# An eight-phase trunk on one core: the order of the program from another timing model

## The chip, the cores and the metric

The kernel runs on one core of a Trainium2 chip. The metric is the device time of one execution in microseconds (us). TensorE (PE) multiplies matrices, VectorE (DVE) and ScalarE (ACT) do elementwise work and reductions, GpSimd (POOL) makes masks, and SyncE (SP) issues the DMAs. Each engine takes its instructions strictly in the order of the program for that engine and waits by semaphores for the others.

## The reference

512 tokens of width 1024 pass through eight sublayers. Each is `x + post_gain * rms_norm(f(rms_norm(x)))`, with these `f` in order: FFN, gated DeltaNet, cross-attention to 256 memory tokens, FFN, FFN, SSD (Mamba-2), cross-attention, FFN. The FFN is a SwiGLU of inner width 2816. The two recurrences, cut to what matters:

```python
# gated DeltaNet, per head and chunk
sol = triangular_solve(eye + a_mat, rhs, lower=True, unit_diagonal=True)
u, wk = sol[..., :dv], sol[..., dv:]
v_new = u - wk @ state
o = (qc * exp(G)) @ state + qk @ v_new
state = state * exp(G_end) + k_end.T @ v_new
...
o = rms_norm(o, norm_g) * silu(z);  return o @ w_out

# SSD, per group and chunk
y = (cb * seg) @ xc + (cc @ state) * exp(acum)
state = state * exp(acum_end) + (bc * to_end).T @ xc
...
yz = rms_norm((y + xs * d_skip) * silu(z), per group);  return yz @ w_out
```

All of it is float32.

## The kernel before

`trunk` makes a list of eight phases and `run` walks through it. The hidden state lies in SBUF with tokens on partitions; in front of each phase `features` (L244 to L250) or the FFN's `enter` (L373 to L382) normalises, transposes on PE and splits the result in two float32r parts, `xh` and `xl`. Every weight block of 128 x 1024 is loaded by one DMA of 512 KB into `raw` (three buffers), cast on ACT to `whi` (L129) and subtracted on DVE to `wlo` (L130; five buffers of each). A projection is then three float32r matmuls for each of eight blocks of the contraction (`mm3`, lines L143, L144, L145), into a PSUM bank. There are eight banks: three of tag `a`, two of `s`, two of `c`, one of `f`.

DeltaNet handles its 16 heads in eight pairs. For pair `p`, `front` (L659 to L716) makes masks and decays, `blocks` (L728 to L735) inverts 16 x 16 diagonal blocks on DVE, between two trips through DRAM, and `solve` (L748 to L795) puts the inverse together with small matmuls (L751, L760, L766, L771, L781, L788, L794). `scan` (L813 to L867) then runs four chunks of 128 tokens in sequence: L820 applies the state `S`, L826 the inverse `U`, L835 and L837 make the output, L845 the new state. At its end stand the sum of squares (L858), a reciprocal root of eleven small DVE steps (`rsqrt`, L307 to L312), the scaling (L867), and in `gate` four transposes for each head (L889), the product with `z` (L890) and the split into `oghi` and `oglo` (L893), which are the operands of the out projection. Between `solve(p)` and `scan(p)` the program writes the four projections of pair `p + 1`, eight blocks of three matmuls each, and the projections for `z` behind.

SSD has eight groups with the same frame: the scan's matmuls are L1068, L1071 and L1082, and its gate multiplies by `z` (L1108), squares (L1112), takes a root, scales (L1116) and transposes (L1120) into `sohi` and `solo`.

The order of the instructions is not the order in which they are written. The framework collects all instructions and schedules them: among those that are ready in its own model of time it takes the one with the lowest priority number, which counts up through the program. The kernel shifts these numbers for whole functions: the table `LATER` gives an offset for each name, and the decorator `prio` applies it while the function is written. What is ready when follows from a timing model of the engines. On each engine the program then holds that order, and waits, buffers and semaphores are set by it.

## Time and profile before

| what | value |
|---|---|
| median of 3 runs | 2835.14 us (2828.82 to 2835.72) |
| profiled execution | 2833.57 us |
| its span | 2831.8 us |
| mean granted clock of PE | 0.993 |
| PE busy | 2785.9 us, 98% |
| DVE, ACT, POOL busy | 2071.3, 1512.9, 124.5 us |
| HBM traffic | 112 GB/s over the span |

A row of the timeline gives the start in us, the duration in us, the engine, the line, the operation, `out<-in`, the form and, with `x2`, how many alike follow each other; in brackets stands the idle time ahead of it and what ended it. Matmuls are pipelined: their durations overlap, and the distance between two starts is what one costs. A row of a view of waits gives the waiting line, the one it waited for, and then the sum in us, the number of times and the longest. A row of the view by stretches gives the stretch and its length, then the busy time and count of PE, PE's weight loads, DVE, ACT and POOL, then PE's granted clock, the DMA share and GB/s.

### The profile page before, as it was taken

What the parts mean: (1) busy time and instruction counts of PE and PEld (TensorE: products, weight loads), DVE (VectorE), ACT (ScalarE), POOL (GpSimd) and SP (SyncE); (2) the same over time, 40 slices, a digit from 0 to 9 for tenths busy, and PEclk for the clock granted to TensorE, in tenths of its full rate; (3) what the DMA queues carried; (4) which work ended last, traced back from release to release, by engine and by line L of the source; (5) the groups of instructions that cost most, each with busy time, mean ns of one, the idle gap of its engine ahead of it and who ended that gap; (6) DMA issues with size and microseconds to landing.
All of it is one profiled execution on the core that took longest, in us unless ns stands there. A gap on an engine that the chain in (4) does not pass through costs nothing.

```text
span 2831.8 us, 45624 instructions
## 1 busy us (share of the span) xinstructions
PE 2785.9 (98%) x17648; PEld 2453.5 (87%) x17648; DVE 2071.3 (73%) x4057; ACT 1512.9 (53%) x2814; POOL 124.5 (4%) x141
## 2 busy tenths in 40 slices
PE   8999999999999999999999999999999999999998
PEld 7999987788888887999988999888888888799997
DVE  8887777767666564887778887777667766588776
ACT  5444477666575574544445444576554656454433
POOL 0000001000000000000000000003212200000000
PEclk9999999999999999999999999999999999999999
DMA  6333433232323432433343332433233363233233
GB/s 215 106 105 105 160 111 103 62 100 81 94 71 121 168 116 73 143 100 102 97 156 127 98 112 90 152 121 108 85 104 106 103 217 112 75 113 112 93 109 105
DMA packets 125913, 320.71 MB, mean 113 GB/s; under 512 B 27472, under 2 KB 46672, under 8 KB 125184
## 3 DMA queue, kind: packets, MB, share of 16 engines
q1 hardware_dynamic: 125696, 317.80, 34.6%
q8 instruction: 139, 2.28, 0.3%
q14 instruction: 78, 0.64, 0.1%
HBM read 293.01 MB, written 24.74 MB: 112 GB/s over the span
## 4 chain that ended last, share of the span: by engine, by line
PE 86%; DVE 7%; ACT 3%; DMA 2%; issue 1%; SPq 0%; DVEq 0%; POOL 0%; ACTq 0%; POOLq 0%
PE ps_a L143 16%; PE ps_a L144 16%; PE ps_a L145 16%; PE ps_s L144 4%; PE ps_s L145 4%; PE ps_s L143 4%; PE ps_c L143 2%; PE ps_c L145 2%; PE ps_c L144 2%; PE ps_f L145 2%; PE ps_f L144 2%; PE ps_f L143 2%; DVE wlo L130 1%; PE ps_c L1068 1%; PE ps_s L1237 1%
## 5 line engine op out<-in xcount | busy, mean ns | idle before, releaser
L143 PE MATMUL ps_a<-xh,whi 128*128 128x256 f32 (+1 forms) x2368 | 754.8, 321 | 2.0 <-ACT xh L381 1.7
L144 PE MATMUL ps_a<-xl,whi 128*128 128x256 f32 (+1 forms) x2368 | 755.4, 320 | 0.1
L145 PE MATMUL ps_a<-xh,wlo 128*128 128x256 f32 (+1 forms) x2368 | 752.3, 319 | 0.0
L143 PEld LDWEIGHTS ps_a<-xh,whi 128*128 128x128 f32 x2368 | 453.5, 192 | 30.3 <-ACT xh L381 2.6
L144 PEld LDWEIGHTS ps_a<-xl,whi 128*128 128x128 f32 x2368 | 455.0, 192 | 26.4 <-DVE xl L382 0.5
L145 PEld LDWEIGHTS ps_a<-xh,wlo 128*128 128x128 f32 x2368 | 454.4, 192 | 23.9
L130 DVE TENSOR_TENSOR wlo<-raw,whi 128x1024 fp32r<-128x1024 f32 x278 | 339.8, 1224 | 159.2 <-ACT whi L129 157.2
L129 ACT CAST whi<-raw 128x1024 fp32r<-128x1024 f32 x278 | 289.1, 1043 | 224.5 <-PE ps_a L144 139.1
L137 ACT CAST whi<-h 128x1024 fp32r<-128x1024 f32 x168 | 175.6, 1048 | 204.3 <-PE ps_a L144 150.3
L138 DVE TENSOR_TENSOR wlo<-h,whi 128x1024 fp32r<-128x1024 f32 x168 | 205.3, 1224 | 88.7 <-ACT whi L137 87.7
L492 ACT CAST bh<-raw 128x512 fp32r<-128x512 f32 x80 | 49.7, 621 | 169.0 <-DMA raw<-ffn_in 140.5
L144 PE MATMUL ps_s<-wlo,hhi 128*128 128x512 f32 x352 | 138.0, 392 | 0.0
L143 PE MATMUL ps_s<-whi,hhi 128*128 128x512 f32 x352 | 137.8, 392 | 0.0
L145 PE MATMUL ps_s<-whi,hlo 128*128 128x512 f32 x352 | 137.2, 390 | 0.0
L143 PE MATMUL ps_c<-whi,hhi 128*128 128x512 f32 x288 | 112.0, 389 | 0.0
L144 PE MATMUL ps_c<-wlo,hhi 128*128 128x512 f32 x288 | 112.0, 389 | 0.0
L145 PE MATMUL ps_c<-whi,hlo 128*128 128x512 f32 x288 | 112.0, 389 | 0.0
L137 ACT CAST whi<-raw 128x1024 fp32r<-128x1024 f32 x80 | 84.0, 1051 | 50.3 <-PE ps_c L145 39.0
L485 DVE TENSOR_TENSOR h<-raw 128x512 f32<-128x512 f32 x80 | 55.1, 689 | 72.1 <-DMA raw<-ffn_in 69.4
L138 DVE TENSOR_TENSOR wlo<-raw,whi 128x1024 fp32r<-128x1024 f32 x80 | 97.4, 1218 | 8.7 <-ACT whi L137 8.7
L512 ACT ACTIVATE h<-h 128x512 f32<-128x512 f32 x80 | 50.6, 633 | 84.3 <-DVE h L509 84.1
L468 ACT CAST hhi<-h 128x512 fp32r<-128x512 f32 x88 | 54.8, 622 | 71.7 <-DVE h L513 43.6
(423 smaller groups left out, 6635.4 us busy)
## 6 DMA issues: line engine op xcount, KB each, us to landing
raw<-ffn_in SPq DMA_DIRECT2D x192, 512.0 KB, 4.2
raw<-ffn_out SPq DMA_DIRECT2D x88, 512.0 KB, 3.5
raw<-dn_in SPq DMA_DIRECT2D x48, 512.0 KB, 3.5
raw<-ssd_in SPq DMA_DIRECT2D x32, 512.0 KB, 3.5
hd<-h SPq DMA_DIRECT2D x24, 512.0 KB, 3.1
h<-hd SPq DMA_DIRECT2D x24, 512.0 KB, 4.2
raw<-dn_out SPq DMA_DIRECT2D x16, 512.0 KB, 3.6
raw<-xa_k SPq DMA_DIRECT2D x16, 512.0 KB, 3.9
```

The lines of the kernel that those rows point to most:

```text
L129: nc.scalar.copy(hi[:, :n], raw[:, :n])
L130: nc.vector.tensor_sub(lo[:, :n], raw[:, :n], hi[:, :n])
L137: nc.scalar.copy(hi, raw)
L138: nc.vector.tensor_sub(lo, raw, hi)
L143: mm(ps, lhs[0], rhs[0], start=first, stop=False)
L144: mm(ps, lhs[0], rhs[1], start=False, stop=False)
L145: mm(ps, lhs[1], rhs[0], start=False, stop=last)
L468: self.t.nc.scalar.copy(hi, x)
L485: sub(T1, u[:, a], g[:, a])
L492: nc.scalar.copy(b22[0], u[:, b])
L512: nc.scalar.activation(gt, gt, AF.Silu)
L1068: nc.tensor.matmul(py[:, e * 64:e * 64 + 64], st["gp"][e][:, c, :], st["xt"][:, c, e * 64:e * 64 + 64], start=True, stop=True)
```

## The change

One argument of the tile context changes. The timing model that the scheduler consults while it orders the program is now the framework's timeline simulation of the engines, and no longer its default model.

```diff
--- before.py
+++ after.py
@@ -1425,7 +1425,7 @@
     nc = _bacc.Bacc("TRN2", target_bir_lowering=False, num_devices=1)
     ap = {n: nc.dram_tensor(n, list(x.shape), F32, kind="ExternalInput").ap() for n, x in arrays.items()}
     ap["out"] = nc.dram_tensor("out", [T, D], F32, kind="ExternalOutput").ap()
-    with tile.TileContext(nc) as tc:
+    with tile.TileContext(nc, schedule_with_timeline_sim=True) as tc:
         trunk(tc, nc, ap)
     res = run_bass_kernel_spmd(nc, [arrays], core_ids=[0])
     return np.asarray(res.results[0]["out"]).reshape(1, T, D)
```

The instructions are the same by name and number: 16552 matmuls, 4054 on DVE, 2392 on ACT, 136 on POOL and 677 DMAs. Only ACT's loads of function tables, which are put in once the order stands, go from 96 to 75. On PE 54% of the matmuls keep their place, the others move by 20 places in the mean and by some 300 at most; on DVE 21%, on ACT 25%, on SP 59% keep theirs. A small matmul is followed by a projection's matmul 524 times in the order before and 261 times now.

PE, the scan of DeltaNet's pair 1, before (names are `out<-weights and data`; `w`, `we`, `o`, `S` belong to the scan, `xh`, `xl`, `whi`, `wlo` to projections):

```order
L837 MATMUL ps_c<-w,gp 128x128 x2
L845 MATMUL ps_c<-we,ktok 128x256
L143 MATMUL ps_a<-xh,whi 128x512
L145 MATMUL ps_a<-xh,wlo 128x512
L144 MATMUL ps_a<-xl,whi 128x512
L143 MATMUL ps_a<-xh,whi 128x512
L145 MATMUL ps_a<-xh,wlo 128x512
L820 MATMUL ps_c<-S,u 128x256
```

The same scan now:

```order
L837 MATMUL ps_c<-w,gp 128x128 x2
L845 MATMUL ps_c<-we,ktok 128x256
L820 MATMUL ps_c<-S,u 128x256
L826 MATMUL ps_c<-o,U 128x128 x2
L835 MATMUL ps_c<-S,u 128x256
L837 MATMUL ps_c<-w,gp 128x128 x2
L845 MATMUL ps_c<-we,ktok 128x256
```

The projections that stood between the steps have moved ahead of the scan. At the end of pair 0's scan, just ahead of this, L889 now follows the last L837 with nothing between, as in the next place.

PE, the end of pair 7's scan, the last of DeltaNet, before (62 projection matmuls, most of them on the memory tokens of the following phase, stand between L837 and the first L889; here are the first of them):

```order
L835 MATMUL ps_c<-S,h 128x256
L145 MATMUL ps_a<-xh,wlo 128x256
L143 MATMUL ps_a<-xh,whi 128x256
L144 MATMUL ps_a<-xl,whi 128x256
L145 MATMUL ps_a<-xh,wlo 128x256
L143 MATMUL ps_a<-xh,whi 128x256
L144 MATMUL ps_a<-xl,whi 128x256
L145 MATMUL ps_a<-xh,wlo 128x256
L837 MATMUL ps_c<-w,gp 128x128 x2
L143 MATMUL ps_a<-xh,whi 128x256
```

And now (`oghi` is the output of the gate, so the last row is the out projection):

```order
L845 MATMUL ps_c<-we,ktok 128x256
L820 MATMUL ps_c<-S,h 128x256
L826 MATMUL ps_c<-o,U 128x128 x2
L835 MATMUL ps_c<-S,h 128x256
L837 MATMUL ps_c<-w,gp 128x128 x2
L889 MATMUL ps_c<-const,o 128x128 x8
L143 MATMUL ps_s<-whi,oghi 128x512
```

Those projections now stand ahead of the last chunk, and the transposes of the gate follow directly on the scan.

PE, the end of SSD's last group, before (78 projection matmuls stand between L1071 and L1120):

```order
L1068 MATMUL ps_c<-xt,gp 128x64 x4
L1071 MATMUL ps_c<-sS,h 128x256
L145 MATMUL ps_a<-xh,wlo 128x256
L143 MATMUL ps_a<-xh,whi 128x256
L144 MATMUL ps_a<-xl,whi 128x256
```

And now:

```order
L145 MATMUL ps_a<-whi,xl 128x512
L1068 MATMUL ps_c<-xt,gp 128x64 x4
L1071 MATMUL ps_c<-sS,h 128x256
L1120 MATMUL ps_c<-const,y 128x128 x8
L143 MATMUL ps_s<-whi,sohi 128x512
```

Here too the gate's transposes follow directly, and the out projection directly on them.

## The prediction

> **What bounds the kernel now.** I read the busy shares first, then what TensorE (PE) waited for, then the timeline around the two recurrences, since the change moves no work and only order can matter.
>
> ```profile
> PE 2785.9 (98%) x17648; PEld 2453.5 (87%) x17648; DVE 2071.3 (73%) x4057; ACT 1512.9 (53%) x2814; POOL 124.5 (4%) x141
> PE ps_c L379 <- DVE u L373: 14.8, 9, 8.8
> PE ps_c L1120 <- DVE y L1116: 4.5, 5, 1.7
> PE ps_s L379 <- DVE u L373: 4.4, 1, 4.4
> PE ps_c L889 <- DVE o L867: 1.9, 3, 1.2
> PE ps_s L781 <- DVE T L772: 1.7, 1, 1.7
> ```
>
> PE is busy for 98% of the 2831.8 us span, so about 46 us are idle. Of these 8.8 and 4.4 lie at the start of the program, where the first tokens are normalised; the next rows are the gates of the two recurrences (L1120, L889) and the solve (L781). The gain that an order could bring by filling idle time is at most these 46 us, and the start's 13 cannot be filled. What an order can lose is larger: every chain that the projections cover now.
>
> A busy PE can still be slow, and the order sets that too. Durations overlap, so I price by the distance from one start to the next.
>
> ```profile
> 546.33 0.39 PE L143 MATMUL ps_a<-xh,whi 128*128 128x512 f32 x1
> 546.56 0.40 PE L144 MATMUL ps_a<-xl,whi 128*128 128x512 f32 x1
> ...
> 549.34 0.49 PE L144 MATMUL ps_a<-xl,whi 128*128 128x512 f32 x1
> 549.67 0.27 PE L751 MATMUL ps_s<-const,T 128*128 128x128 f32 x1
> 549.70 0.48 PE L145 MATMUL ps_a<-xh,wlo 128*128 128x512 f32 x1
> 550.01 0.82 PE L751 MATMUL ps_s<-const,T 128*128 128x128 f32 x6
> ```
>
> Among their like, 512-column projections start 0.23 us apart (546.33 to 546.56). Right behind a small transpose one holds the engine 0.33 us (549.34 to 549.67) and 0.31 us (549.70 to 550.01). So each change from a small matmul to a projection costs about 0.09 us.
>
> **The chains that projections cover.** One chunk of DeltaNet's scan, as it runs now:
>
> ```profile
> 540.36 0.61 PE L837 MATMUL ps_c<-w,gp 128*128 128x128 f32 x4
> 540.80 0.60 PE L845 MATMUL ps_c<-we,ktok 128*128 128x256 f32 x2
> 542.61 0.59 PE L820 MATMUL ps_c<-S,u 128*128 128x256 f32 x2
> 543.24 0.61 DVE L822 SCALAR_TENSOR_TENSOR o<-ps_c,ncol,o 128x128 f32<-128x128 f32 x2
> 544.21 0.60 PE L826 MATMUL ps_c<-o,U 128*128 128x128 f32 x4
> 544.85 0.42 DVE L832 COPY w<-ps_c 128x256 f32<-128x256 f32 x1 [1.00 <-PE ps_c L826]
> 545.33 0.71 PE L837 MATMUL ps_c<-w,gp 128*128 128x128 f32 x4
> ```
>
> From L837 to the next L837 is 4.97 us. Its own matmuls fill about 2.2 us (L837 0.44 us to the start of L845, L845 and L820 some 0.43 each as they hold the engine, L826 0.44, the L835 beside it 0.43); the rest, 2.8 us, is filled with projections. After the last chunk comes the norm and the gate:
>
> ```profile
> 546.08 0.62 ACT L841 ACTIVATE qs<-ps_c,eG 128x128 f32<-128x128 f32 x2 [0.59 <-PE ps_c L837]
> 548.05 1.28 ACT L698 ACT_TABLE_LOAD   x1
> 548.06 0.17 DVE L860 TENSOR_TENSOR so<-so,rq 128x8 f32<-128x8 f32 x1 [0.91 <-ACT junk L858]
> 551.54 2.74 DVE L867 TENSOR_SCALAR o<-o,rsy 128x128 f32<-128x128 f32 x8
> 552.24 0.30 PE L889 MATMUL ps_c<-const,o 128*128 128x128 f32 x1 [1.18 <-DVE o L867]
> 554.86 0.73 DVE L890 SCALAR_TENSOR_TENSOR z<-ps_c,cw,z 128x512 f32<-128x512 f32 x1
> 555.63 0.62 ACT L893 CAST oghi<-z 128x512 fp32r<-128x512 f32 x1 [1.49 <-DVE z L890]
> ```
>
> From the last L837 (545.33) to the first L889 are 6.9 us, of which PE has 0.45 of its own; from L889 to the end of the cast, 556.25, another 4.0, with some 2 us in which neither transposes nor anything else of the chain needs PE. SSD's last group has the same shape:
>
> ```profile
> 2279.71 0.65 PE L1071 MATMUL ps_c<-sS,h 128*128 128x256 f32 x2
> 2282.64 0.42 ACT L1112 ACTIVATE sjunk<-y 128x256 f32<-128x256 f32 x1 [0.47 <-DVE y L1108]
> 2282.96 0.19 ACT L1112 ACTIVATION_READ_ACCUMULATOR sjunk<-y 128x1 f32 x1
> 2285.07 0.41 ACT L1112 ACTIVATE sjunk<-y 128x256 f32<-128x256 f32 x1
> 2289.77 1.14 DVE L1116 TENSOR_SCALAR y<-y,rsy 128x256 f32<-128x256 f32 x4
> 2290.27 0.87 PE L1120 MATMUL ps_c<-const,y 128*128 128x128 f32 x6 [0.56 <-DVE y L1116]
> ```
>
> L1071 to L1120 takes 10.6 us, and PE goes on with 256-column projections throughout. Part of it is others' work on ACT (the fourth L1112 starts 2.43 us after the first; three before it, at 0.42 plus 0.19 for reading the sum, need 1.8) and on DVE. Undisturbed I put it at 8.4 us, of which some 7.5 behind L1071's own work.
>
> **The change, part by part.** No instruction is added; the counts on every engine agree, except that ACT's loads of function tables fall from 96 to 75. At 1.28 us each (the row at 548.05) that is 27 us of an engine that is 53% busy. On PE's path they count for little: I price this at nothing, covered by PE's own work, and, without that cover, at 1.28 us for each load that stands in a chain.
>
> *Loads of weights.* The 677 DMAs stay too, 59% of SP's rows in the same place.
>
> ```profile
> raw<-dn_in SPq DMA_DIRECT2D x48, 512.0 KB, 3.5
> ```
>
> One load lands 3.5 us after its issue and is then cast and split. Three raw and five split buffers run ahead of PE, and PE takes 5.5 us for the 24 matmuls of one block (24 x 0.23), so I price the moved loads at nothing; a load that comes late by the reuse of a buffer would cost up to its 3.5 us, and with SP's order so close to the old one I expect few.
>
> *Gain: fewer changes of kind.* In PE's order a projection follows a small matmul 524 times before and 261 times now: 263 x 0.09 = 24 us less. This is a real saving, since PE is the bound. From below: 32 of them are 256-column ones, which no row here prices apart, so 231 x 0.08 = 18 us at least.
>
> *Gain: old stalls in the recurrences.* The L1120, L889 and L781 rows above are 8.1 us. I let them go whole; from the other side they stay.
>
> *Loss, place A: DeltaNet's pairs 0 and 1.* The new order runs the projections in blocks of 15 to 25 between steps of a chain, and then has none left. At pair 0's end L889 stands directly behind the last L837: 6.9 - 0.45 = 6.4 us of idle PE, and 2.0 more until the out projection has its operand. Then pair 1's scan runs three chunks with no projection between: 3 x 2.8 = 8.4 us. Sum 16.8. Behind L889 wait all of the following projections, since PE takes its instructions in order.
>
> *Loss, pairs 6 and 7.* Pair 6's second chunk has only 2.6 us of PE work: 4.97 - 2.6 = 2.4 us, and as much, 2.2, is taken for its neighbour, whose norm is short of cover: 4.6. Pair 7 ends with a bare chunk and then L889 directly behind L837 and the last out group behind that (place B): 2.8 + 6.4 + 2.0 = 11.2 us.
>
> *Loss, place C: SSD's last group.* L1120 stands directly behind L1071, and the out group directly behind L1120: 7.5 + 1.0 (the cast, on the pattern of 555.63) = 8.5 us.
>
> *Loss, elsewhere.* Laying the same hops (from the rows above) over the whole order, wherever less PE work stands between a step and its successor than the hop needs, gives 79.7 us of stalls now and 27.8 before; the four places make 41.1 of the difference of 52. The other 11 are runs of up to 24 transposes (L379) through two PSUM banks at the start of FFN1 and FFN2, and small deficits in the solve. I take 8, because the FFN1 to FFN2 boundary idles 5 us already.
>
> *The clock.* Long idle time has a second price.
>
> ```profile
> 495.00:499.00 4.00, 2.33 (x25) 1.35 (x24) 3.93 (x11) 1.99 (x8) 1.12 (x2) 0.96 0.00 0
> 499.00:512.00 13.00, 13.00 (x77) 8.85 (x76) 5.34 (x15) 6.97 (x24) 0.00 (x0) 0.50 0.00 0
> 922.00:935.00 13.00, 13.00 (x83) 11.70 (x80) 0.90 (x3) 4.15 (x10) 0.00 (x0) 0.50 0.18 61
> 1501.00:1506.00 5.00, 1.50 (x10) 0.85 (x8) 4.79 (x9) 1.25 (x4) 0.00 (x0) 0.96 0.80 260
> 1506.00:1512.00 6.00, 4.26 (x20) 4.05 (x20) 4.38 (x7) 3.22 (x6) 0.00 (x0) 0.50 0.16 64
> ```
>
> Behind a stretch in which PE worked 1.5 of 5 us the granted clock is 0.50 for some 6 us (1506 to 1512); twice it stays there for 13 us (499, 922). An episode of 6 us loses about 3, one of 13 about 6.5, so before pays 16 in all. Places A (twice), B and C each idle 6 us or more: four episodes of 3 make 12, if A's do not merge into long ones. Of the old three I expect the one at 922 (small matmuls of the solve) to change and the one at 499 (the gates, before any scan) to stay. Net I take +3, between -4 (all old ones gone, 12 paid) and +20 (nothing gone, A held at half speed over 13 us as at 922).
>
> [...]
>
> *Sum.* 16.8 + 4.6 + 11.2 + 8.5 = 41.1; + 8 elsewhere; + 3 clock; - 24 changes; - 8 old stalls: +20. The count over the whole order gives 52 + 3 - 24 = +31, and does not assume that every old stall goes. I take +25, the middle. Against the profiled execution's 2833.57 us that is 2858.6; the median of the three runs is 2835.14, 1.57 above it, so 2860.
>
> **The rivals.**
>
> *Faster: the engine-bound reading.* The 24 us of changes are certain by count; the stalls are not. The chains before run among other work on DVE and ACT, and with fewer bystanders they shorten: if the hops are 40% shorter, 52 becomes 31 us, and where the order lays a second chain beside the first (the solve of pair 1 beside the scan of pair 0) that may fill 20 of them. Then 11 - 24 = -13: 2822. It wins from the point where all new stalls together fall under 24. For it: in the chunk above, L826 starts 0.36 us after L822 has ended and L832 has 1.00 us of idle ahead of it, so the hops hold waits that are not the chain's own. Against it: A's and B's bare runs leave nothing but the chain itself, and the 6.4 us are mostly a row of dependent 0.17 us steps like L860.
>
> *No change.* Half of the stalls come true: 26 + 3 - 24 = +5, 2840. It decides if the 21 table loads that go stood in chains, at 1.28 us each; the one at 548.05 stands beside L860 and off the chain, which speaks against it.
>
> *Much slower: the clock.* In place A the solve and scan of pairs 0 and 1 run on for some 40 us with PE half idle. If the clock stays at 0.50 as in 922 to 935 over all of A and over B and C, another 20 to 30 us are lost: 2860 + 25 = 2885, and up to 2900. For it: two of three episodes here lasted 13 us. Against it: an idle PE at half speed loses little while the chain waits on DVE.
>
> *The change does nothing.* Excluded: of PE's matmuls 46% stand at another place.
>
> **How the numbers follow.** A measurement here tells from no change what is over 0.3%, 8.5 us. Forecast (+10 to +45) 0.56; much slower 0.14; no change (within 8.5) 0.15; faster 0.15. So faster 0.15, same 0.15, slower 0.70. The forecast's own range is 2845 to 2880. For 8 in 10 the range goes down to 2824, which takes in no change and the upper part of faster, and up to 2894 for most of the clock's case.
>
> **What would show it.** PE's idle rows should name L889 <- DVE o L867 with single waits of 5 to 7 us (A and B) and L1120 <- DVE y L1116 with one of about 7; the scan's L820, L826 and L837 should turn up with about 8 us in sum in pair 1. PE's busy time should fall by some 20 us in spite of the longer span. The clock should show at least three half-speed stretches near A, B and C. If PE's idle time stays under 60 us the forecast's stalls are wrong; if busy time does not fall, the price of the changes is; if DMA weights (whi, wlo) head PE's waits, the new order starves on loads, which I have not priced.

## The result, and the profile after

| | before | changed |
|---|---|---|
| median of 4 runs | 2834.26 us (2828.82 to 2835.72) | 2971.60 us (2967.34 to 2981.61) |
| ratio | | 1.0493, 95% interval 1.0463 to 1.0524 |
| profiled execution, span | 2833.57, 2831.8 us | 2981.61, 2979.8 us |
| granted clock of PE, mean | 0.993 | 0.972 |

The change makes the kernel 4.9% slower, 137 us, where 25 us were forecast and 2894 was the end of the range. The profiled execution of the changed kernel is the slowest of its four, 10 us over the median, so what follows is worked out on 148 us (2979.8 - 2831.8).

The page and the waits of PE in the changed kernel (waiting line, the line it waited for, sum in us, times, longest):

```profile
PE 2829.8 (95%) x17648; PEld 2496.5 (84%) x17648; DVE 2080.1 (70%) x4057; ACT 1478.7 (50%) x2793; POOL 128.3 (4%) x141
...
PE ps_c L379 <- DVE u L373: 18.5, 4, 10.5
PE ps_c L889 <- DVE o L867: 16.0, 3, 7.6
PE ps_c L1120 <- DVE y L1116: 13.5, 3, 9.7
PE ps_c L244 <- DVE xl L250: 10.6, 4, 5.3
PE ps_c L837 <- DVE w L832: 9.1, 8, 2.1
PE ps_a L143 <- ACT sz L1103: 7.5, 2, 4.3
PE ps_a L143 <- DVE h L286: 7.3, 6, 4.0
PE ps_s L751 <- DMA T<-td: 6.4, 5, 2.5
PE ps_s L788 <- ACT W L782: 4.5, 7, 1.9
```

PE is idle for 150 us (2979.8 - 2829.8) and was for 46. Its busy time rose too, by 44 us, with the same matmuls. (Half-clock time is, from here on, the time that a trace shows at a granted clock of 0.50; a chain is bare where no projection stands behind its steps to cover their waits.) The next two fences have the view by stretches for DeltaNet and then SSD, from the first matmul behind the phase before to the first of the next; of the kernel before, then of the changed one:

```profile
360.50:994.00 633.50, 628.12 (x3945) 515.37 (x3944) 431.35 (x1178) 407.65 (x1027) 32.20 (x48) 0.98 0.33 102
1836.00:2332.70 496.70, 487.60 (x2584) 410.31 (x2583) 358.79 (x800) 290.99 (x479) 91.16 (x88) 1.00 0.36 119
```

```profile
366.50:1092.00 725.50, 658.15 (x3966) 540.01 (x3965) 435.94 (x1181) 396.51 (x1017) 33.18 (x48) 0.93 0.29 91
1943.80:2477.40 533.60, 500.20 (x2593) 422.87 (x2592) 360.42 (x801) 278.97 (x473) 93.93 (x88) 0.97 0.35 114
```

DeltaNet takes 92 us more and SSD 37, together 129 of the 148; no other phase differs by more than 6 us. In DeltaNet 62 us of it are idle time (67.3 against 5.4), in SSD 24, and the clock fell from 0.98 to 0.93 and from 1.00 to 0.97.

To split idle time, clock and changes of kind I gave each matmul the distance to the next start and took off the usual distance of its kind at full clock in the kernel before. What is over goes to "clock" while the granted clock is 0.50 (up to once the usual distance), to "stall" if over 0.2 us is left, to "change" if a projection stands behind a small matmul, else to "rest". The sum of the usual distances is the floor.

| us | stall | change | clock | rest |
|---|---|---|---|---|
| before | 48.6 | 55.7 | 11.3 | 43.3 |
| changed | 173.5 | 29.3 | 50.5 | 52.0 |
| difference | +124.9 | -26.4 | +39.2 | +8.7 |

The four make 146 of the 148 us. Where stall, clock and rest meet depends on the usual distance that is taken: with the median of each tile and form, stalls rise by 111 us, the clock's part by 42 and rest by 20, while the changes stay at -26. The forecast places are there. Place A, the end of pair 0, as PE shows it:

```profile
562.66 1.09 PE L837 MATMUL ps_c<-w,gp 128*128 128x128 f32 x4
570.70 1.94 PE L889 MATMUL ps_c<-const,o 128*128 128x128 f32 x8 [6.95 <-DVE o L867]
573.27 0.47 PE L813 MATMUL ps_c<-const,u 128*128 128x128 f32 x1 [0.63 <-DVE z L890]
```

L889 stood idle 6.95 us (6.4 forecast). At place C it was 9.74 us against 7.5, and the timeline of all engines shows where the rest came from:

```profile
2446.67 0.65 PE L1071 MATMUL ps_c<-sS,h 128*128 128x256 f32 x2
...
2448.28 1.22 DVE L1108 TENSOR_TENSOR y<-y,sz 128x1024 f32<-128x1024 f32 x1
2451.07 1.04 ACT L129 CAST whi<-raw 128x1024 fp32r<-128x1024 f32 x1 [4.41 <-DMA raw<-xa_q]
2452.02 0.41 ACT L1112 ACTIVATE sjunk<-y 128x256 f32<-128x256 f32 x1
...
2457.06 1.30 PE L1120 MATMUL ps_c<-const,y 128*128 128x128 f32 x5 [9.74 <-DVE y L1116]
```

L1108 ends at 2449.5, but the squares L1112 on ACT start at 2452.0: the order has put a cast of weights (L129) ahead of them, and that cast waited 4.41 us for its DMA. 2.5 us of the stall are a queue, not the chain. The same in the middle of SSD, around one gate; first the two steps of the root in the kernel before (at its last group), then the changed kernel:

```profile
2286.34 0.16 DVE L1113 TENSOR_SCALAR sso<-sso 128x4 f32<-128x4 f32 x1
2286.54 0.17 DVE L307 TENSOR_SCALAR rsy<-sso 128x4 int32<-128x4 int32 x1
```

```profile
2122.69 0.17 DVE L1113 TENSOR_SCALAR sso<-sso 128x4 f32<-128x4 f32 x1
2125.03 1.23 DVE L130 TENSOR_TENSOR wlo<-raw,whi 128x1024 fp32r<-128x1024 f32 x1 [2.17 <-ACT whi L129]
2126.49 1.23 DVE L130 TENSOR_TENSOR wlo<-raw,whi 128x1024 fp32r<-128x1024 f32 x1 [0.23 <-ACT whi L129]
2127.63 0.16 DVE L307 TENSOR_SCALAR rsy<-sso 128x4 int32<-128x4 int32 x1
...
2129.34 0.58 ACT L1103 ACTIVATE sz<-ps_a 128x512 f32<-128x512 f32 x1
...
2129.97 0.50 PE L143 MATMUL ps_a<-whi,sohi 128*128 128x512 f32 x1 [4.30 <-ACT sz L1103]
```

From L1113 to L307, 0.20 us before, are 4.9 us here: two splits of weights (L130) stand between them, and they wait for casts on ACT. Beside it a PSUM bank of tag `a` is held until ACT comes to L1103, and PE stands for 4.30 us.

### The profile page after: what moved, and what is told of

Same layout as the page of the kernel before. It is cut to its first block, busy times and chain, and to the rows that moved or that the text cites. A ratio compares the mean times of both kernels' runs of the same rounds, so it can differ in the third digit from the quotient of the medians.

```text
span 2979.8 us, 45592 instructions
## 1 busy us (share of the span) xinstructions
PE 2829.8 (95%) x17648; PEld 2496.5 (84%) x17648; DVE 2080.1 (70%) x4057; ACT 1478.7 (50%) x2793; POOL 128.3 (4%) x141
## 4 chain that ended last, share of the span: by engine, by line
PE 54%; DVE 4%; ACT 2%; DMA 2%; issue 1%; POOL 0%; DVEq 0%; ACTq 0%; SPq 0%; POOLq 0%
PE ps_a L143 10%; PE ps_a L144 10%; PE ps_a L145 10%; PE ps_s L143 4%; PE ps_s L144 4%; PE ps_s L145 4%; PE ps_c L144 2%; PE ps_c L143 2%; PE ps_c L145 2%; PE ps_f L143 1%; PE ps_f L144 1%; PE ps_f L145 1%; PE ps_a L1261 1%; PE ps_s L1237 1%; DVE gp L1044 1%
## 5 line engine op out<-in xcount | busy, mean ns | idle before, releaser
L143 PE MATMUL ps_a<-xh,whi 128*128 128x256 f32 (+1 forms) x2368 | 743.1, 319 | 11.5 <-DVE h L286 3.3
L130 DVE TENSOR_TENSOR wlo<-raw,whi 128x1024 fp32r<-128x1024 f32 x278 | 341.5, 1231 | 184.4 <-ACT whi L129 181.6
L129 ACT CAST whi<-raw 128x1024 fp32r<-128x1024 f32 x278 | 289.8, 1044 | 262.1 <-PE ps_a L144 165.6
L143 PE MATMUL ps_f<-s2h,whi 128*128 128x256 f32 x320 | 90.6, 283 | 0.0
L144 PE MATMUL ps_f<-s2l,whi 128*128 128x256 f32 x320 | 90.6, 283 | 0.0
```

The source lines that it names most:

```text
L129: nc.scalar.copy(hi[:, :n], raw[:, :n])
L130: nc.vector.tensor_sub(lo[:, :n], raw[:, :n], hi[:, :n])
L143: mm(ps, lhs[0], rhs[0], start=first, stop=False)
L144: mm(ps, lhs[0], rhs[1], start=False, stop=False)
```

## The experiments

In all of them an order is held by ordering edges between neighbours on one engine, which use no semaphore; what is not held is ordered by the timing model that is named. Read from the held orders, the 46% of PE's matmuls that change place move by 44 places in the mean; 20 is the mean over all of them. The code below is cut to what matters, and in the first runs the list of matmuls is made while the program is written:

```diff
-        trunk(tc, nc, ap)
+        trunk(tc, nc, ap), hold_order(tc, nc)
+
+def hold_order(tc, nc):
+    info = mybir.DependencyInfo(mybir.DependencyClass.NoSync, mybir.DependencyReason.DATA)
+    every = [i for b in nc.cur_f.blocks for i in b.instructions]
+    for e, s in ORDERS.items():
+        made = [i for i in every if e in str(i.engine) and type(i).__name__ not in NOT]
+        row = [made[k] for k in rank(s)]
+        for a, b in zip(row, row[1:]):
+            tc.add_manual_dep(b, a.name, info, reason="order held")
```

### PE's order and the order of the others, crossed

New PE order, default model for the rest (`ORDERS` holds PE of the changed kernel, context without the argument):

> The changed kernel's order of PE's 16552 matmuls, held by ordering edges without semaphores, while the default timing model orders VectorE, ScalarE, GpSimd and the DMAs around it. Theory A (PE's order alone carries the loss): within 20 us of the changed kernel, 2950 to 2990 us. Rival B (a good part comes from the orders of VectorE and ScalarE, whose late casts and gates PE waits for: sz L1103 7.5, h L286 7.3, xl L250 10.6 us and part of the scan): 2880 us or less. In between, both.

Old PE order, timeline simulation for the rest (`ORDERS` holds PE of the kernel before, context with the argument):

> The reverse: the order of PE's matmuls from the kernel before, held by ordering edges, everything else ordered by the timeline simulation. Theory A: 2825 to 2850 us, no change against before. Rival B: 2870 us or more.

| median, us | rest by the default model | rest by the timeline simulation |
|---|---|---|
| PE's old order | 2834 | 3005.95 (ratio 1.0586, 1.0565 to 1.0607) |
| PE's new order | 2955.82 (1.041, 1.039 to 1.043) | 2971.6 |

By the first column theory A holds: PE's order alone costs 4.1 of the 4.9%. But the second run refutes it as stated: with PE in its old order the kernel is slower than with both new. The orders fit each other in pairs. By phase (DeltaNet from the first L673 of its pair 2, which is how the expectations count it, and SSD from its first L1068, each to the next phase's first L1237; the middle column is the time from the program's start to the first L1237 behind DeltaNet, and so has pairs 0 and 1 in it):

| us, profiled execution | DeltaNet from pair 2 | start to first L1237 | SSD |
|---|---|---|---|
| before | 533.8 | 1028.4 | 441.0 |
| new PE order, rest default | 640.6 | 1135.3 | 448.1 |
| old PE order, rest timeline | 582.0 | 1093.8 | 513.3 |
| changed | 641.6 | 1130.1 | 480.4 |

So there are two losses in two places. Up to the end of DeltaNet, PE's new order costs 107 us beside the default model's order of the rest, as much as the whole change (102). Beside the timeline simulation's order of the rest, which costs 65 us there by itself, it adds only 36: the two prices do not add up. In SSD the new PE order costs 7 us, place C (L1120 waits once, for 7.3 us), and the order of the others 32 on top; beside PE's old order they cost 72.

### DeltaNet alone

The next two runs hold PE's order of the kernel before, except in DeltaNet, places 2526 to 5564. The first has the new order there:

```diff
-    row = old
+    row = old[:2526] + new[2526:5564] + old[5564:]
```

> The kernel before with PE's order of the changed kernel held inside DeltaNet alone (positions 2526 to 5564 of 16552), the old order of PE elsewhere, the default model for the other engines. Theory (DeltaNet's PE order makes the larger part by itself): DeltaNet 640 us, 2935 to 2955 us in all. Rival (the phases push each other's loss): 2900 us or less, or 2970 or more.

2940.09 us, ratio 1.0365 (1.0334 to 1.0396), and DeltaNet took 643.2 us from pair 2 on. As expected: 102 us (the kernel before had 2837.81 beside it) from PE's order in this one phase, and the later phases stay at their old times (SSD 442.7).

The second keeps the small matmuls in their old order among each other:

```diff
-    row = old[:2526] + new[2526:5564] + old[5564:]
+    small, proj = iter(small_of(old[2526:5564])), iter(projections_of(new[2526:5564]))
+    mixed = [next(proj) if is_projection(i) else next(small) for i in new[2526:5564]]
+    row = old[:2526] + mixed + old[5564:]
```

> As the run on DeltaNet alone, but the small matmuls keep their old order among each other, and only the projections stand as in the changed kernel: the same places of PE's order are projections, in the same long runs. Theory E (the long runs of projections with bare chains behind them make the loss): DeltaNet within 20 us of the run on DeltaNet alone, 620 to 660 us. Rival F (the new order of the small steps among each other makes it, since solve and scan of two pairs stand in each other's way): DeltaNet 580 us or less.

3055.01 us, ratio 1.078 (1.074 to 1.0819). DeltaNet's scans and solves end 217 us later than before (first L1237 at 1245.5 against 1028.4). F falls as it was put: without the new order of the small steps DeltaNet is slower, not faster. E holds in its sign and not in its size, for this mixture is worse than the new order as it is: with the steps in the old order L889 waits ten times instead of three, six times for more than 5 us.

```profile
PE ps_c L889 <- DVE o L867: 46.6, 10, 8.4
```

Beside the long runs the new order of the small steps takes back 115 us, about half of their price. The reverse, the new small steps with the projections at their old places, was not tried.

### Which engine's order costs SSD its 32 us

PE's order of the changed kernel in each, with ScalarE's, with VectorE's, and with both; the rest by the default model (`ORDERS` has two or three entries):

> PE's and ScalarE's orders of the changed kernel held, VectorE, GpSimd and DMAs ordered by the default model. With PE's order alone SSD took 448 us, in the changed kernel 480. If ScalarE's order makes these 32 us (PE waited for sz L1103 7.5 us and sohi): SSD 470 us or more and 2965 to 2990 us in all. If not: SSD 440 to 455, 2945 to 2962 us.

> PE's and VectorE's orders of the changed kernel held, ScalarE, GpSimd and DMAs ordered by the default model. If VectorE's order makes SSD's 32 us (its casts L130 queue in front of the root L310 to L312 and the scaling L1116): SSD 470 us or more, 2965 to 2990 us in all. If not: SSD 440 to 455, 2945 to 2962 us.

> PE's, ScalarE's and VectorE's orders of the changed kernel held together; only GpSimd and the DMAs are ordered by the default model. If holding an order is the same as having it, this is the changed kernel again: 2960 to 2985 us, SSD 475 to 485. If it is over 2990, as with PE and ScalarE (2993) or PE and VectorE (3021), the place of GpSimd's work and of the DMAs carries a part, or the edges cost something themselves.

| held | all, us | ratio | SSD, us |
|---|---|---|---|
| PE | 2955.82 | 1.041 | 448.1 |
| PE and ScalarE | 2993.23 | 1.0556 (1.0536 to 1.0576) | 475.2 |
| PE and VectorE | 3021.18 | 1.0659 (1.0637 to 1.0681) | 490.3 |
| all three | 2979.14 | 1.0529 (1.0497 to 1.0561) | 481.0 |

Held together, the three orders are the changed kernel again within 0.4% (ratios 1.0529 and 1.0493), so holding an order costs nothing that matters. Each of the two alone brings SSD's loss back, and both make the whole kernel slower than the 2990 us that were expected at most. That is not 27 and 42 us that add up. The likely reason, which no run separates, is that casts on ScalarE and splits on VectorE are two ends of one chain (L129 to L130), so that the other engine must follow whichever order is held. The rows above show both ends: at 2451 the gate's squares stand behind a cast that waits for its DMA, at 2125 its root stands behind splits that wait for casts.

### What the half clock costs

The changed kernel with its own PE order, and extra matmuls on a constant in front of the matmuls that stand behind long idle times. The real matmul overwrites what they write.

```diff
+        for _ in range(KEEP.get(n, 0)):
+            nc.tensor.matmul(ps, kw[:, 0:128], kw, start=True, stop=True)
         r = matmul(ps, ...)
```

> The changed kernel in its own PE order, with 934 extra matmuls (128x128 by 128 columns, on a constant) in front of the 71 matmuls that start behind the longest idle times of PE (109 of its 150 us), each written to the place that the real matmul then overwrites. Theory C (idle PE drops the clock, and the low clock is a loss of its own, about 40 us): half-clock time falls from 168 us to under 80 and the time by 20 to 40 us, to 2930 to 2950, though no wait is removed. Rival D (the low clock comes with the small matmuls of solve and scan, or only fills time in which PE would wait anyway): half-clock time stays over 130 us or the time moves by less than 10 us.

3036.05 us, ratio 1.0697 (1.0673 to 1.072); half-clock time 178 us, no less (168 in the changed kernel). That is the sign of rival D and not what C expected, and the trace shows why. Around place B (lines from the extra matmuls' own helper; L1484 is every real matmul):

```profile
1070.86 4.51 PE L1483 MATMUL ps_c<-kw 128*128 128x128 f32 x19
1075.17 1.16 PE L1484 MATMUL ps_c<-w,gp 128*128 128x128 f32 x4
1075.98 17.31 PE L1483 MATMUL ps_c<-kw 128*128 128x128 f32 x80
1093.09 1.93 PE L1484 MATMUL ps_c<-const,o 128*128 128x128 f32 x8
1096.30 0.79 PE L1484 MATMUL ps_s<-whi,oghi 128*128 128x512 f32 x1 [1.28 <-ACT oghi L897]
```

```profile
1071.50:1100.00 28.50, 27.22 (x120) 25.96 (x120) 10.55 (x32) 5.63 (x12) 0.00 (x0) 0.50 0.21 64
```

PE is busy for 27.2 of 28.5 us, with 80 matmuls in one row, and the clock stays at 0.50; so it does in rows of 56 (12.0 us from 1125.6) and 42 (9.0 us from 2167.4). Matmuls of 128 columns did not end a half clock here. But where the clock was full they kept it so. At place A, where the changed kernel was at half clock for 10.2 us, 73 of them ran at the full clock but for the first 0.3 us, the end of an older stretch; at place C, where it was for 13.7 us, all of 105:

```profile
565.00:573.50 8.50, 8.50 (x76) 8.50 (x76) 5.94 (x24) 7.45 (x26) 2.58 (x4) 0.98 0.19 65
2505.60:2517.40 11.80, 11.80 (x107) 11.77 (x106) 7.51 (x21) 4.04 (x10) 0.00 (x0) 1.00 0.58 179
```

At half clock each took 0.216 us, so they also delayed what stood behind. The same with 512 columns:

> As the run with extra matmuls before, now with 404 of them and 512 columns each (256 in front of L837), as a projection has, and 67 places, lengths cut to the idle time less 0.2 us (86 us in all). Theory C2 (the clock goes by how dense the work on the array is; matmuls of 128 columns do not count as work, those of 512 do): half-clock time falls from 168 us to under 90, and the time to 2930 to 2955 us. Rival D (the low clock belongs to the small matmuls of solve and scan, not to the idle time): half-clock time stays over 130 us, and the time at 2965 us or more.

Half-clock time fell to 75 us and the mean clock rose to 0.988, as C2 has it (that matmuls of 128 columns do not count at all is not borne out by the two rows above), but the time was 2992.25 us, ratio 1.0554 (1.0532 to 1.0575), 20 more than the changed kernel. The 404 matmuls cost some 90 to 103 us (floor and rest of the account rose by so much, depending on the usual distance taken for them), and stalls fell by only 45 to 54. The reason is a finding in itself:

```profile
2139.46 5.97 PE L1490 MATMUL ps_a<-kw 128*128 128x512 f32 x18 [4.16 <-ACT sz L1109]
```

The extra matmul needs no data, only the PSUM bank, and it waited 4.16 us as the real one had (4.30). So that wait was for the bank and not for an operand. At 33 of the 67 places the extra matmuls had such a wait of 0.3 us or more; these places have 44.8 us of the changed kernel's idle time, the 34 others 61.0. A third run puts extra matmuls only at places of the second kind, and fewer than the wait holds:

> The changed kernel with extra matmuls of 512 columns only at the 22 places where, in the run before, they started without a wait of their own (so PE waits there for the data of the real matmul and not for its PSUM bank), and only as many as fill some 60% of the wait, at the long ones all but 1.2 us: 181 of them, 37 us in all, so that none should delay the real matmul. Theory C3 (the half clock follows idle time and is a loss on top of it, some 25 us of the changed kernel's loss at these places): half-clock time under 120 us, and 2945 to 2960 us against 2972. Rival (the clock's loss lies inside waits that are there anyway): 2966 to 2980 us, with less half-clock time all the same.

2972.53 us, ratio 1.0479 (1.045 to 1.0509), half-clock time 89 us, clock 0.985. Half the half-clock time is gone and the time is that of the changed kernel, 2971.6. The rival holds, with a reserve: the account says that the clock gave 20 us back and that the extra matmuls took some 10 more than the stalls they filled, and the changed kernel's profile is itself 10 us over its median. So by this estimate the clock's own price at these 22 places is at most some 10 to 20 us, and the runs do not separate it from the waits.

### Fewer changes of kind, without bare chains

The kernel before, where on PE small matmuls of one PSUM tile that stand within 12 places are brought to the place of the last, and a lone projection between two groups is moved ahead (one place of the order, as an example):

```diff
-L751  L144  L751  L145  L751 x6
+L144  L145  L751 x8
```

> The kernel before with its default order, where on PE alone small matmuls that write the same PSUM tile within 12 places are brought together, and a single projection matmul between two groups of small ones moves ahead of them: changes from a small matmul to a projection fall from 524 to 332, with no chain delayed by more than about 0.3 us a step. Theory (a change costs about 0.1 us of PE and is paid in full): 15 to 20 us faster than before, 2815 to 2822. Rival (the chains have no slack and each delay of a step is paid): no change or slower, 2835 or more.

2888.84 us, ratio 1.0179 (1.0156 to 1.0201), slower by 49 us. The changes cost 38.5 us instead of 55.7 by the account, the 17 us that were expected; stalls rose by 47 and the clock's part by 14. 14.2 us of PE's waits are for L814, 22 times: L813 makes four transposes into one bank, and brought together each waits until L814 has read the one before. The theory falls and its rival holds.

The second run leaves L813 where it was:

> The kernel before with groups of small matmuls of one PSUM tile brought together within 12 places, as in the run with fewer changes, but the transposes L813 left where they were (each of them waits for ScalarE's L814 on the one before it, which cost 17 us there) and no projection moved otherwise: 524 changes become 398. Theory (0.1 us for each change, chains not delayed otherwise): 8 to 14 us faster than before, 2821 to 2828 at a level of 2835. Rival (any delay of a step is paid, since the solve and scan chains have no slack): slower by 10 us or more.

2857.66 us, ratio 1.008 (1.0055 to 1.0104), slower by 21 us, and the rival holds once more. Again the changes gave their part (55.7 to 44.2), and again the delays took more:

```profile
PE ps_s L788 <- ACT W L782: 6.3, 12, 1.4
...
PE ps_c L1249 <- DVE p L1246: 3.7, 2, 1.9
...
PE ps_s L771 <- DVE T L772: 2.8, 1, 2.8
```

None of these waits is one of a bare chain's end; they are hops inside of solve and of attention (L788 and L1249 waited 0 and 0.3 us before), which a few projections had just covered. No experiment beats the kernel before.

## Why the prediction was wrong, point by point

The direction and the two phases were right, the size was not: the step that failed is the sum of the losses, in two of its terms. "Elsewhere", which with the old stalls taken off came to nothing, was some 67 us of stalls, and the clock, priced at 3, was 39.

- **Changes of kind, -24.** Measured -26.4. This term stands, in a change that loses 137 us.
- **Places A, pairs 6 and 7, C: 41.1.** Stalls by the account there: A 8.9 + 11.3, pair 6 11.7, B 15.3, C 10.7, sum 57.9. The ends of chains were priced well (6.95 and 7.58 us for L889 against 6.4), place C less so, since ACT's queue stood in the chain (with PE's new order and the default model for the rest L1120 waited 7.3, as forecast). Pair 6 was the worst guess, 11.7 against 4.6.
- **Elsewhere, 8; old stalls, -8.** This is the large miss: net nothing was forecast, and of the +125 us of stalls some 67 lie outside the four places. Three things were not in the price.
  - First, hops were laid over PE's order as if a chain's step ran when its operand was there, and that count (27.8 before, 79.7 now) fell short even of what PE's order does alone. With PE's new order and the rest by the default model, the account with medians has 145 us of stalls, against 47 before and 157 in the changed kernel; 90 of these 98 us stand ahead of the first L1237, where the forecast's places had 32.6 (A and pairs 6 and 7), so most of the miss is DeltaNet's. On ACT and DVE a step also waits behind whatever stands ahead in that engine's order (2.5 us at the squares of 2452, 4.7 us at the root of 2127, both in SSD); how much of DeltaNet's part that makes is not shown.
  - Second, the forecast priced the new orders of ACT and DVE at nothing but table loads (21 fewer, which no run prices alone). The crossed runs put 32 us of SSD there.
  - Third, waits for PSUM banks: the extra matmuls without operands found them at 33 places with 44.8 us of idle time, some of them at the four places, where the forecast had 8 for banks and small deficits together.
- **The clock, +3.** The account has +39; the upper bound of 20 was too low. The forecast took four episodes of 6 us from four long idle times. Those lasted 10.2 and 3.4 us at A and 13.7 each at B and C, and in all there were 23 half-clock stretches instead of 4, 168 us in sum instead of 41:

```profile
550.60:564.30 13.70, 13.15 (x70) 9.97 (x70) 2.81 (x8) 5.04 (x17) 0.00 (x0) 0.50 0.01 1
586.00:600.00 14.00, 8.70 (x43) 5.15 (x41) 10.47 (x47) 5.40 (x21) 0.00 (x0) 1.00 0.04 6
1062.60:1076.30 13.70, 5.88 (x17) 4.58 (x18) 10.37 (x32) 5.24 (x10) 0.00 (x0) 0.50 0.35 118
```

  What begins each is not shown. The first was at half clock with PE busy for 13.15 of 13.70 us, and in the 5.6 us ahead of it PE was busy for 5.40. The second, pair 1's bare scan with waits of 0.4 to 0.9 us at most of its steps, ran at 1.00. The third is place B, mostly waiting. How much of the 39 us would be lost at full clock too, as waiting, the runs leave open.
- **Loads of weights, nothing.** Wrong in one place at least: the cast at 2451 waited 4.41 us for its DMA, and with it the gate.
- **The rivals.** "Much slower: the clock" had the nearest time, 2885 to 2900, and its mechanism is a part of the loss. The row at 586, at 1.00, speaks against its picture, since the forecast feared half speed there.
- **The signs that were named.** L889 and L1120 head PE's idle rows as named, next to L379. PE's busy time did not fall by 20 us but rose by 44, though the changes paid: matmuls at half clock stay busy for longer (0.216 us against 0.114 for the extra ones above). So that sign could not test the price of a change.

What the traces show of the half clock besides: in the row 1071.50:1100.00 dense small matmuls did not end it in some 24 us (1070.9 to 1095.0), while behind the first 512-column projection, at 1096.3, full clock was back after 5.0 us, at 1101.3. Each half-clock stretch of the changed kernel but the one at its end lasts once, twice, three or four times 3.41 us.

What stays open: which hops of DeltaNet's chains were too short in the forecast, how the 67 us of stalls outside the four places divide between queues and banks (a third bank for tag `c` was not tried), and why the timeline simulation prefers these orders.

## What to carry to other kernels

An order of one engine was worth something here only with the orders of the others: crossing PE's old order with the new order of the rest gave 3005.95 us, the worst of all four. Before pricing a reordering, lay the chain over every queue that it passes (which cast stands ahead of it on ACT, which split on DVE, who holds its PSUM bank), not over PE alone. This kernel at 98% PE has spent its slack: 126 fewer changes of kind, each of which paid out as reckoned, still lost 21 us in the end to delays of at most a few projections.

## What the runs showed of the hardware

- In the run with 934 extra matmuls, dense matmuls of 128x128 by 128 columns left the clock as they found it: 80 in a row at 0.50 for 17.3 us, 105 in a row at 1.00 for 11.8 us. Half-clock time was 178 us with 128-column fillers and 75 us with 512-column ones (fewer, and not at all of the same places).
- In the kernels before and after, each half-clock stretch that does not run into the program's end lasted a multiple of 3.41 us: 13.65, 13.65 and 6.83 before, and 3.41, 6.83, 10.24 or 13.65 in the changed kernel. Around the row of 80 the clock was at 0.50 for 34.2 us, from 1067.1 to 1101.3.
- At full clock such a 128-column matmul held PE for 0.114 us (73 in 8.33 us) and one with 512 columns for 0.227 (18 in a row of 4.25 us, of which the last takes 0.39): four times the columns for twice the time.
- A matmul without operands to wait for served as a probe for banks: what it waited for was its PSUM bank (4.16 of 4.30 us at one place, nothing of 6.95 at L889), and so it told a wait for a bank from a wait for data, which the view of waits names alike.
